# Three pairs of k-tiles for two in a kernel that takes seven block products for eight, with the weight sums written in place

## The chip, the cores and the metric

The kernel runs on one core of a Trainium2 chip. The metric is the device time of one execution in microseconds (us); it is the median of several runs.

## The reference

Four layers over 256 tokens of width 2048, in float32: an S5 layer with a gated unit, a dilated attention layer, each with a SwiGLU feed-forward network (FFN) behind it, and then two mixer layers (retention, differential attention, a linear recurrence). What this case is about is the gated unit and the two FFNs:

```python
D_MODEL = 2048
D_FF = -(-8 * D_MODEL // (3 * 256)) * 256          # 5632

def swiglu_ffn(h, w_gate_up, w_down):
    gate, up = jnp.split(h @ w_gate_up, 2, axis=-1)
    return (jax.nn.silu(gate) * up) @ w_down

# gated unit of the S5 layer
val, gate = jnp.split(g @ w_glu, 2, axis=-1)
return (val.astype(f32) * jax.nn.sigmoid(gate.astype(f32))).astype(u.dtype)
```

## The kernel before

All weights are float32 in HBM and are read once. For a matrix product each operand is split in two float32r parts, `hi` (a cast on ACT) and `lo` (the difference, on DVE), and a product is three matmuls of 128x128 by 128x512: hi by hi, hi by lo, lo by hi. The activations lie transposed in `act_hi` and `act_lo` as 16 k-tiles of 128 rows by 256 tokens; the tokens are two halves of 128. PSUM has four banks `psg` for these products and four banks `psm` for the rest.

`gemm` (L55) is the plain product of 512 columns. `Strassen.gemm_pair` (L136) takes 1024 columns as two halves of 512 (the gate and the up columns of one chunk, or two neighbouring column blocks of `w_down`). For four of the k-tiles, as two pairs, it uses the Winograd form of Strassen's scheme: the two token halves, the two k-tiles of a pair and the two column halves make a 2 by 2 block product, which takes seven block products (L180 to L187) for eight. Their left operands are blocks of the activations or the sums made by `forms` (L109), made once for each set of activations; the right operands are three blocks of the weights (b11, b21, b22) and four sums (t3 = b22 - b12, t1 = b12 - b11, t2 = b22 - t1, t4 = b21 - t2) made by `total` (L153, its instruction L155) into a pool tile `wt` with three buffers. `split` (L127) makes `whi` (L132) and `wlo` (L133) of each of the seven; `product` (L158) issues the matmuls (L166 to L168); `kept` copies four intermediate results out of PSUM. The raw weights of this part are one tile `wraw4` with one buffer, loaded by L148.

The other twelve k-tiles go the direct way, in six groups of two (L204 to L222): a group is loaded into a tile of the pool `wraw`, which has two buffers (WB), each of its k-tiles is split into one `whi` and one `wlo` tile (four buffers each), and 12 matmuls follow on each. In the last group the order is by token half, so the banks c21 and c22 are done first. Then four adds (L230) put the kept parts back, or, for the down product, the caller adds them to `x` one by one (L376).

Between the seven products and the direct groups `jobs` runs what is waiting in `k.jobs`. In `ffn` this is `turn`: the gated chunk `midt` is transposed into `mid` (L269 to L274), and for the first chunk of a block of four the sums `mf` for the down product are made.

The order of instructions on each engine isn't the order of the program: a planner, which runs when the program is built, starts an instruction when its operands and its buffers are there by its own clock, and earlier lines go first. Buffers of a pool tile with one name go round. At the chip each engine then runs its list in that order.

`ffn` (L323) has eleven chunks of 512 in blocks of four, four and three: a first chunk by `gemm`, ten gate/up pairs, and two down pairs for each block. `glu` has three pairs.

## Time and profile before

| | us |
|---|---|
| median of 3 runs | 3208.32 (3207.38 to 3209.45) |
| profiled execution | 3209.36 |
| its span | 3207.6 |
| PE busy | 3137.0 |
| DVE busy | 2277.0 |
| ACT busy | 1728.8 |

The mean granted clock of the TensorE is 0.996 of full speed. Lines with an L number are those of the kernel; numbers of buffers are left out of names, so `wraw` stands for the pool of the direct groups and for `wraw4` alike. A time that begins a row of a timeline is in us from the start of the span.

### The profile page before, as it was taken

Reading aid. Unit: us, or ns where it says so; the run is one execution under the profiler, and the core shown is the slowest. Engines: PE = TensorE matmul, PEld = TensorE weight load, DVE = VectorE, ACT = ScalarE, POOL = GpSimd, SP = SyncE. Lnnn points to the kernel's source line nnn. Section 1 sums busy time; section 2 is a strip of 40 time slices with the busy share of each in tenths; the row PEclk is TensorE's granted clock in tenths of the full one; section 3 lists DMA queues with packets and bytes.
Section 4 is the critical chain, followed back from the end, with each engine's and each line's share of the span. In section 5 each row is a group of like instructions: output and inputs, shape, how many; then the busy total and the mean of one; then the engine's idle time right before and its main releaser. Section 6 shows DMA issues by size and latency. Waiting matters only on the chain.

```text
span 3207.6 us, 43406 instructions
## 1 busy us (share of the span) xinstructions
PE 3137.0 (98%) x16872; PEld 2671.6 (83%) x16883; DVE 2277.0 (71%) x3421; ACT 1728.8 (54%) x2335; POOL 13.8 (0%) x23
## 2 busy tenths in 40 slices
PE   4999999999999999999999999999999999999998
PEld 4788888888888888888888888888889898899887
DVE  8967777777777665756768777777858566575564
ACT  6355655455555655545455555545556455564463
POOL 1000000000000000000000000000000000000000
PEclk9999999999999999999999999999999999999999
DMA  3265655665555555454565565566555557456554
GB/s 55 85 216 171 210 182 186 209 210 194 200 197 178 171 168 177 163 189 158 168 204 186 195 201 184 182 207 210 184 162 166 184 152 221 158 165 202 155 182 170
DMA packets 343215, 573.96 MB, mean 179 GB/s; under 512 B 55073, under 2 KB 106785, under 8 KB 342177
## 3 DMA queue, kind: packets, MB, share of 16 engines
q1 hardware_dynamic: 309344, 561.91, 53.5%
q10 hardware_dynamic: 33664, 9.28, 1.4%
q8 instruction: 132, 2.16, 0.3%
q14 instruction: 75, 0.61, 0.1%
HBM read 568.51 MB, written 2.62 MB: 178 GB/s over the span
## 4 chain that ended last, share of the span: by engine, by line
PE 91%; DVE 3%; ACT 3%; DMA 2%; issue 0%; SPq 0%; ACTq 0%; another core or an unknown queue 0%; DVEq 0%
PE psg L71 14%; PE psg L69 14%; PE psg L70 14%; PE psg L220 11%; PE psg L221 11%; PE psg L222 11%; PE psg L166 4%; PE psg L167 3%; PE psg L168 3%; PE psm L269 1%; PE psg L399 1%; DMA wraw<-in_w_in 1%; DVE S L399 1%; PE psm L1044 1%; DVE sc L399 1%; ACT VW L399 1%
## 5 line engine op out<-in xcount | busy, mean ns | idle before, releaser
L43 DVE TENSOR_TENSOR wlo<-wraw,whi 128x1024 fp32r<-128x1024 f32 (+1 forms) x560 | 628.1, 1131 | 467.9 <-ACT whi L42 466.6
L42 ACT CAST whi<-wraw 128x1024 fp32r<-128x1024 f32 (+1 forms) x560 | 540.8, 978 | 640.1 <-PE psg L71 377.1
L133 DVE TENSOR_TENSOR wlo<-wraw,whi 128x1024 fp32r<-128x1024 f32 x509 | 608.4, 1222 | 279.5 <-ACT whi L132 277.1
L69 PE MATMUL psg<-whi,act_hi 128*128 128x512 f32 (+1 forms) x2144 | 802.8, 374 | 0.9 <-DVE act_lo L399 0.7
L71 PE MATMUL psg<-whi,act_lo 128*128 128x512 f32 (+1 forms) x2144 | 796.4, 372 | 4.1 <-DVE act_lo L279 4.1
L70 PE MATMUL psg<-wlo,act_hi 128*128 128x512 f32 (+1 forms) x2144 | 796.2, 371 | 0.8 <-DVE wlo L43 0.8
L132 ACT CAST whi<-wraw 128x1024 fp32r<-128x1024 f32 x509 | 522.8, 1055 | 488.7 <-DMA wraw<-in_w_gate_up 168.5
L220 PE MATMUL psg<-whi,act_hi 128*128 128x512 f32 x1616 | 630.8, 390 | 0.8 <-ACT whi L132 0.8
L221 PE MATMUL psg<-wlo,act_hi 128*128 128x512 f32 x1616 | 628.9, 389 | 0.8 <-DVE wlo L133 0.8
L222 PE MATMUL psg<-whi,act_lo 128*128 128x512 f32 x1616 | 628.8, 389 | 0.0
L71 PEld LDWEIGHTS psg<-whi,act_lo 128*128 128x128 f32 x2144 | 403.2, 188 | 59.9 <-DVE act_lo L279 5.0
L69 PEld LDWEIGHTS psg<-whi,act_hi 128*128 128x128 f32 x2144 | 403.6, 188 | 55.6 <-issue 1.3
L70 PEld LDWEIGHTS psg<-wlo,act_hi 128*128 128x128 f32 x2144 | 403.7, 188 | 53.7 <-DVE wlo L43 1.5
L220 PEld LDWEIGHTS psg<-whi,act_hi 128*128 128x128 f32 x1616 | 303.4, 188 | 63.6 <-ACT whi L132 1.2
L221 PEld LDWEIGHTS psg<-wlo,act_hi 128*128 128x128 f32 x1616 | 303.4, 188 | 63.4 <-DVE wlo L133 1.1
L222 PEld LDWEIGHTS psg<-whi,act_lo 128*128 128x128 f32 x1616 | 303.3, 188 | 63.1
L132 ACT CAST whi<-wt 128x1024 fp32r<-128x1024 f32 x140 | 147.7, 1055 | 119.7 <-PE psg L222 101.7
L133 DVE TENSOR_TENSOR wlo<-wt,whi 128x1024 fp32r<-128x1024 f32 x140 | 170.8, 1220 | 50.4 <-ACT whi L132 50.3
L155 DVE TENSOR_TENSOR wt<-wraw 128x1024 f32<-128x1024 f32 x70 | 84.3, 1220 | 8.4 <-DMA wraw<-in_w_down 6.7
L155 DVE TENSOR_TENSOR wt<-wraw,wt 128x1024 f32<-128x1024 f32 x70 | 85.5, 1221 | 1.1
L168 PE MATMUL psg<-whi,act_lo 128*128 128x512 f32 x210 | 82.0, 390 | 0.0
L167 PE MATMUL psg<-wlo,act_hi 128*128 128x512 f32 x210 | 81.9, 390 | 0.0
(359 smaller groups left out, 2931.6 us busy)
## 6 DMA issues: line engine op xcount, KB each, us to landing
wraw<-in_w_gate_up SPq DMA_DIRECT2D x320, 512.0 KB, 4.7
wraw<-in_w_down SPq DMA_DIRECT2D x176, 512.0 KB, 5.1
wraw<-in_w_in SPq DMA_DIRECT2D x96, 768.0 KB, 4.7
wraw<-in_w_q SPq DMA_DIRECT2D x48, 1024.0 KB, 5.1
wraw<-in_w_kv SPq DMA_DIRECT2D x32, 1024.0 KB, 5.5
wraw<-in_w_in SPq DMA_DIRECT2D x32, 1024.0 KB, 5.0
wraw<-in_w_out SPq DMA_DIRECT2D x32, 1024.0 KB, 5.1
wraw<-in_w_glu SPq DMA_DIRECT2D x48, 512.0 KB, 4.7
```

What stands on the lines that cost most here:

```text
L42: k.act_at = nc.scalar.copy(hi[:, :n, :cw], raw[:, a:a + n, :cw]).ins
L43: k.dve_at = nc.vector.tensor_tensor(lo[:, :n, :cw], raw[:, a:a + n, :cw], hi[:, :n, :cw].bitcast(F32), ALU.subtract).ins
L69: nc.tensor.matmul(o, a, wh, start=n == 0, stop=False)
L70: nc.tensor.matmul(o, a, wl, start=False, stop=False)
L71: k.mm = nc.tensor.matmul(o, b, wh, start=False, stop=n == total - 1).ins
L132: k.act_at = nc.scalar.copy(hi, src).ins
L133: k.dve_at = nc.vector.tensor_tensor(lo, src, hi.bitcast(F32), ALU.subtract).ins
L167: nc.tensor.matmul(o, a, wl[:, q], start=False, stop=False, skip_group_check=True)
L168: k.mm = nc.tensor.matmul(o, b, wh[:, q], start=False, stop=q == 1, skip_group_check=True).ins
L220: nc.tensor.matmul(o, a, wh[:, n], start=False, stop=False, skip_group_check=True)
L221: nc.tensor.matmul(o, a, wl[:, n], start=False, stop=False, skip_group_check=True)
L222: k.mm = nc.tensor.matmul(o, b, wh[:, n], start=False, stop=g == last and j == 1, skip_group_check=True).ins
```

## The change

The seven products take three pairs of k-tiles in all pairs but the down pairs of layer 1, which keep two; five direct groups remain for six. A block of weights is now two pieces, of two pairs and of one (`sizes`), each with its own raw tile, its own sums and its own `whi` and `wlo` tile, of which the second uses half. t1 is written over b11, t3 over b12, t4 over t2; t2 has a tile of its own for each piece. The product with b21 stands ahead of that with t4. The sums of the activations are made by `fill` in pieces too, and the room for that is no longer two `wt` buffers but one buffer of `wraw`; the piece of two pairs is filled after the first chunk of a block, that of one pair after the second. `midt` has one buffer for two, and so has `sil` in layer 1.

```diff
@@ -103,32 +103,36 @@
     def __init__(self, k, pool):
         self.k, self.pool = k, pool
 
-    def block(self):
-        return self.pool.tile([128, 2, 512], F32, name="wt", bufs=3)
-
-    def forms(self, xT, kt0, name):
+    def new_forms(self, kt0, name, sizes=(2, 1)):
+        return (kt0, sizes, *(self.pool.tile([128, 4, sum(sizes), 128], F32R, name=f"{name}_{n}") for n in ("hi", "lo")))
+
+    def fill(self, forms, xT, groups=None):
 
         k, nc = self.k, self.k.nc
-        xh, xl = (x[:, kt0:kt0 + 4, :] for x in xT)
-        hi, lo = (self.pool.tile([128, 4, 2, 128], F32R, name=f"{name}_{n}") for n in ("hi", "lo"))
-        x = self.block().rearrange("p q (i t) -> p (q i) t", i=2)
-        nc.vector.tensor_tensor(x, xh.bitcast(F32), xl.bitcast(F32), ALU.add)
-        x = x.rearrange("p (q i) t -> p q i t", i=2)
-        a11, a12, a21, a22 = (x[:, :, i, t * 128:(t + 1) * 128] for t in range(2) for i in range(2))
-        sm = self.block().rearrange("p a (b t) -> p (a b) t", t=128).rearrange("p (f q) t -> p f q t", q=2)
-        nc.vector.tensor_tensor(sm[:, 0], a21, a22, ALU.add)
-        nc.vector.tensor_tensor(sm[:, 2], a11, a21, ALU.subtract)
-        nc.vector.tensor_tensor(sm[:, 1], sm[:, 0], a11, ALU.subtract)
-        nc.vector.tensor_tensor(sm[:, 3], a12, sm[:, 1], ALU.subtract)
-        nc.scalar.copy(hi, sm)
-        nc.vector.tensor_tensor(lo, sm, hi.bitcast(F32), ALU.subtract)
-        return kt0, hi, lo
+        kt0, sizes, hi, lo = forms
+        for g in range(len(sizes)) if groups is None else groups:
+            m, q0 = sizes[g], sum(sizes[:g])
+            room = k.wraw.tile([128, 4, 512], F32, name="wraw")
+            xh, xl = (x[:, kt0 + 2 * q0:kt0 + 2 * (q0 + m), :] for x in xT)
+            h, l = (f[:, :, q0:q0 + m, :] for f in (hi, lo))
+            x = room[:, 0:m].rearrange("p q (i t) -> p (q i) t", i=2)
+            nc.vector.tensor_tensor(x, xh.bitcast(F32), xl.bitcast(F32), ALU.add)
+            x = x.rearrange("p (q i) t -> p q i t", i=2)
+            a11, a12, a21, a22 = (x[:, :, i, t * 128:(t + 1) * 128] for t in range(2) for i in range(2))
+            sm = room[:, 2:2 + m].rearrange("p a (b t) -> p (a b) t", t=128).rearrange("p (f q) t -> p f q t", q=m)
+            nc.vector.tensor_tensor(sm[:, 0], a21, a22, ALU.add)
+            nc.vector.tensor_tensor(sm[:, 2], a11, a21, ALU.subtract)
+            nc.vector.tensor_tensor(sm[:, 1], sm[:, 0], a11, ALU.subtract)
+            nc.vector.tensor_tensor(sm[:, 3], a12, sm[:, 1], ALU.subtract)
+            nc.scalar.copy(h, sm)
+            nc.vector.tensor_tensor(l, sm, h.bitcast(F32), ALU.subtract)
 
     def split(self, src):
 
         k, nc = self.k, self.k.nc
-        hi = k.whi.tile([128, 2, 512], F32R, name="whi")
-        lo = k.wlo.tile([128, 2, 512], F32R, name="wlo")
+        m = src.shape[1]
+        hi = k.whi.tile([128, 2, 512], F32R, name="whi")[:, :m, :]
+        lo = k.wlo.tile([128, 2, 512], F32R, name="wlo")[:, :m, :]
         k.act_at = nc.scalar.copy(hi, src).ins
         k.dve_at = nc.vector.tensor_tensor(lo, src, hi.bitcast(F32), ALU.subtract).ins
         return hi, lo
@@ -139,33 +143,42 @@
 
 
         k, nc = self.k, self.k.nc
-        kt0, sh, sl = forms
+        kt0, sizes, sh, sl = forms
+        pairs = sum(sizes)
         xh, xl = xT
-        raw = self.pool.tile([128, 2, 2, 2, 512], F32, name="wraw4")
-        for n, c0 in enumerate(cols):
-            for q in range(2):
-                r0 = row0 + (kt0 + 2 * q) * 128
-                nc.sync.dma_start(raw[:, q, :, n, :], W[r0:r0 + 256, c0:c0 + 512].rearrange("(i p) c -> p i c", p=128))
-        b11, b12, b21, b22 = (raw[:, :, i, n, :] for i in range(2) for n in range(2))
+        raws = []
+        for g, m in enumerate(sizes):
+            raws.append(self.pool.tile([128, m, 2, 2, 512], F32, name=f"sraw{g}"))
+            for n, c0 in enumerate(cols):
+                for q in range(m):
+                    r0 = row0 + (kt0 + 2 * (sum(sizes[:g]) + q)) * 128
+                    nc.sync.dma_start(
+                        raws[g][:, q, :, n, :], W[r0:r0 + 256, c0:c0 + 512].rearrange("(i p) c -> p i c", p=128)
+                    )
+        b11, b12, b21, b22 = ([r[:, :, i, n, :] for r in raws] for i in range(2) for n in range(2))
         c22, c21, c11, c12 = (k.psg.tile([128, 512], F32, name="psg") for _ in range(4))
         blocks = {"A11": (0, 0), "A12": (1, 0), "A22": (1, 1)}
 
-        def total(a, b):
-            t = self.block()
-            nc.vector.tensor_tensor(t, a, b, ALU.subtract)
-            return t
+        def less(outs, a, b):
+            for g in range(len(sizes)):
+                nc.vector.tensor_tensor(outs[g], a[g], b[g], ALU.subtract)
+            return outs
 
         def product(o, form, w, start):
-            wh, wl = self.split(w)
-            for q in range(2):
-                if form in blocks:
-                    i, t = blocks[form]
-                    a, b = (x[:, kt0 + 2 * q + i, t * 128:(t + 1) * 128] for x in xT)
-                else:
-                    a, b = (x[:, int(form[1]) - 1, q, :] for x in (sh, sl))
-                nc.tensor.matmul(o, a, wh[:, q], start=start and q == 0, stop=False, skip_group_check=True)
-                nc.tensor.matmul(o, a, wl[:, q], start=False, stop=False, skip_group_check=True)
-                k.mm = nc.tensor.matmul(o, b, wh[:, q], start=False, stop=q == 1, skip_group_check=True).ins
+            q0 = 0
+            for m, src in zip(sizes, w):
+                wh, wl = self.split(src)
+                for q in range(m):
+                    if form in blocks:
+                        i, t = blocks[form]
+                        a, b = (x[:, kt0 + 2 * (q0 + q) + i, t * 128:(t + 1) * 128] for x in xT)
+                    else:
+                        a, b = (x[:, int(form[1]) - 1, q0 + q, :] for x in (sh, sl))
+                    end = q0 + q == pairs - 1
+                    nc.tensor.matmul(o, a, wh[:, q], start=start and q0 + q == 0, stop=False, skip_group_check=True)
+                    nc.tensor.matmul(o, a, wl[:, q], start=False, stop=False, skip_group_check=True)
+                    k.mm = nc.tensor.matmul(o, b, wh[:, q], start=False, stop=end, skip_group_check=True).ins
+                q0 += m
 
         def kept(o, name):
             e = self.pool.tile([128, 512], F32, name=name)
@@ -174,19 +187,21 @@
 
         product(c22, "A11", b11, True)
         p1 = kept(c22, "st_p1")
-        product(c21, "S3", total(b22, b12), True)
+        t1 = less(b11, b12, b11)
+        t3 = less(b12, b22, b12)
+        t2 = less([self.pool.tile([128, m, 512], F32, name=f"wt{g}") for g, m in enumerate(sizes)], b22, t1)
+        product(c21, "S3", t3, True)
         p7 = kept(c21, "st_p7")
-        t1 = total(b12, b11)
-        t2 = total(b22, t1)
         product(c22, "S2", t2, False)
         u2 = kept(c22, "st_u2")
-        product(c21, "A22", total(b21, t2), False)
+        t4 = less(t2, b21, t2)
         product(c11, "A12", b21, True)
+        product(c21, "A22", t4, False)
         product(c22, "S1", t1, False)
         u4 = kept(c22, "st_u4")
         product(c12, "S4", b22, True)
 
-        direct = [kt for kt in kts if not kt0 <= kt < kt0 + 4]
+        direct = [kt for kt in kts if not kt0 <= kt < kt0 + 2 * pairs]
         calls = 1 + len(direct) // 4
         called = 0
 
@@ -322,7 +337,7 @@
 @with_exitstack
 def ffn(ctx, k, layer):
     nc, I = k.nc, k.I
-    work = ctx.enter_context(k.tc.tile_pool(name="ffnw", bufs=2))
+    work = ctx.enter_context(k.tc.tile_pool(name="ffnw", bufs=1))
     st = Strassen(k, ctx.enter_context(k.tc.tile_pool(name="strassen", bufs=1)))
     dff = I["w_down"].shape[1]
     gain = load_gain(k, I["ffn_norm"][layer])
@@ -330,15 +345,16 @@
     rstd = x_stats(k)
     wgu, wd = I["w_gate_up"][layer], I["w_down"][layer]
     nch = dff // 512
-    mforms = []
+    forms = st.new_forms(KT - 6, "xf")
     for s0 in range(0, nch, 4):
         n = min(4, nch - s0)
         mid = act_pair(k, 0)
+        mforms = st.new_forms(0, "mf", (2, 1)[:2 - layer])
         for c in range(s0, s0 + n):
             m = work.tile([128, 2, 512], F32, name="midt")
 
             def silu(t, g):
-                sil = work.tile([128, 512], F32, name="sil")
+                sil = work.tile([128, 512], F32, name="sil", bufs=2 - layer)
                 nc.scalar.activation(sil, g, AF.Silu, scale=rstd[:, t:t + 1])
                 return sil
 
@@ -348,7 +364,7 @@
             if c == 0:
                 pg = gemm(k, xT, kgroups(), wgu, 0, 512)
                 sils = [silu(t, pg[t]) for t in range(2)]
-                forms = st.forms(xT, 12, "xf")
+                st.fill(forms, xT)
                 pu = gemm(k, xT, kgroups(), wgu, dff, 512)
                 for t in range(2):
                     gated(t, pu[t], sils[t])
@@ -357,17 +373,17 @@
                 for t in (1, 0):
                     gated(t, ps[t][1], silu(t, ps[t][0]))
 
-            def turn(m=m, c=c, s0=s0):
+            def turn(m=m, c=c):
                 split_transposed(
                     k, lambda t, i: m[:, t, i * 128:(i + 1) * 128], mid, [4 * (c - s0) + i for i in range(4)]
                 )
-                if c == s0:
-                    mforms.append(st.forms(mid, 0, "mf"))
+                if c - s0 < len(mforms[1]):
+                    st.fill(mforms, mid, (c - s0,))
 
             meanwhile(k, turn)
         for nn in range(0, 4, 2):
             pd, rest = st.gemm_pair(
-                mid, mforms[-1], range(4 * n), wd, s0 * 512, (nn * 512, nn * 512 + 512), apart=True
+                mid, mforms, range(4 * n), wd, s0 * 512, (nn * 512, nn * 512 + 512), apart=True
             )
             for of in (rest, pd):
                 for t in (1, 0):
@@ -933,7 +949,8 @@
         load_x(k)
     k.lo_at = k.sp_at = None
     sig = [sigmoid(t, pg[t]) for t in range(2)]
-    forms = st.forms(gT, 12, "xf")
+    forms = st.new_forms(KT - 6, "xf")
+    st.fill(forms, gT)
     pv = gemm(k, gT, groups, w, 0, 512)
     for t in range(2):
         gated(0, t, pv[t], sig[t])
```

## Rows read from the trace of the kernel before

**Rows 1.** The page: chain of work that ended last, by engine.

```profile
PE 91%; DVE 3%; ACT 3%; DMA 2%; issue 0%; SPq 0%; ACTq 0%; another core or an unknown queue 0%; DVEq 0%
```

**Rows 2.** The chain in order of time: start us, us, what.

```profile
476.10 0.87 PE psm L269 x8
519.22 0.87 PE psm L269 x8
```

**Rows 3.** Timeline of PE in a direct stretch: start us, us, what.

```profile
477.05 0.40 PE L221 MATMUL psg<-wlo,act_hi 128*128 128x512 f32 x1
...
502.90 0.39 PE L221 MATMUL psg<-wlo,act_hi 128*128 128x512 f32 x1
```

**Rows 4.** Busy time by stretch: from:to, us, PE, PEld, DVE, ACT, POOL, clock, DMA.

```profile
509.47:519.05 9.58, 9.58 (x43) 7.84 (x42) 9.58 (x11) 9.01 (x12) 0.00 (x0) 1.00 0.09 24
519.05:552.58 33.53, 33.53 (x153) 27.91 (x152) 24.63 (x26) 13.65 (x15) 0.00 (x0) 1.00 0.74 244
```

**Rows 5.** Timeline of DVE to the next seven products; in brackets idle before, and releaser.

```profile
489.19 1.23 DVE L155 TENSOR_TENSOR wt<-wraw 128x1024 f32<-128x1024 f32 x1 [0.45 <-DMA wraw<-in_w_down]
490.33 1.22 DVE L133 TENSOR_TENSOR wlo<-wraw,whi 128x1024 fp32r<-128x1024 f32 x1
491.47 1.22 DVE L155 TENSOR_TENSOR wt<-wraw 128x1024 f32<-128x1024 f32 x1
492.72 1.23 DVE L155 TENSOR_TENSOR wt<-wraw,wt 128x1024 f32<-128x1024 f32 x1
...
502.59 1.23 DVE L133 TENSOR_TENSOR wlo<-wraw,whi 128x1024 fp32r<-128x1024 f32 x1 [1.49 <-ACT whi L132]
...
507.65 1.21 DVE L155 TENSOR_TENSOR wt<-wraw,wt 128x1024 f32<-128x1024 f32 x1
508.79 0.74 DVE L346 SCALAR_TENSOR_TENSOR midt<-psg,rstd,sil 128x512 f32<-128x512 f32 x1
509.45 0.69 DVE L230 TENSOR_TENSOR psg<-psg,st_p 128x512 f32<-128x512 f32 x1
510.05 0.69 DVE L230 TENSOR_TENSOR psg<-psg,st_u 128x512 f32<-128x512 f32 x1
510.64 1.21 DVE L133 TENSOR_TENSOR wlo<-wt,whi 128x1024 fp32r<-128x1024 f32 x1
```

**Rows 6.** Groups by line over the whole span: count, then busy us, mean ns, idle before.

```profile
L155 DVE TENSOR_TENSOR wt<-wraw,wt 128x1024 f32<-128x1024 f32 x70 | 85.5, 1221 | 1.1
L155 DVE TENSOR_TENSOR wt<-wraw 128x1024 f32<-128x1024 f32 x70 | 84.3, 1220 | 8.4 <-DMA wraw<-in_w_down 6.7 <-DMA wraw<-in_w_gate_up 1.6
```

**Rows 7.** Timeline of ACT in the same direct stretch.

```profile
483.84 2.00 ACT L132 CAST whi<-wraw 128x1024 fp32r<-128x1024 f32 x2 [5.63 <-DMA wraw<-in_w_gate_up]
...
492.58 2.00 ACT L132 CAST whi<-wraw 128x1024 fp32r<-128x1024 f32 x2 [3.62 <-DMA wraw<-in_w_gate_up]
...
501.51 1.05 ACT L132 CAST whi<-wraw 128x1024 fp32r<-128x1024 f32 x1 [1.67 <-PE psg L222]
```

**Rows 8.** Timeline of DVE behind a pair whose job makes the sums `mf`.

```profile
393.68 1.23 DVE L115 TENSOR_TENSOR wt<-act_hi,act_lo 128x1024 f32<-128x1024 f32 x1
...
399.95 1.22 DVE L124 TENSOR_TENSOR mf_lo<-wt,mf_hi 128x1024 fp32r<-128x1024 f32 x1
```

**Rows 9.** Timeline of SP's queue; then GB/s in 40 slices of 466 to 510.

```profile
473.97 0.88 SPq L148 DMA_DIRECT2D wraw<-in_w_down  x2
476.24 4.28 SPq L208 DMA_DIRECT2D wraw<-in_w_gate_up  x4
...
496.25 5.76 SPq L208 DMA_DIRECT2D wraw<-in_w_down  x4
...
GB/s 0 0 0 0 0 0 0 0 171 236 387 341 339 385 404 380 356 372 331 101 97 326 408 147 123 363 397 71 65 330 344 214 19 227 330 246 155 0 0 0
```

**Rows 10.** Timeline of PE behind a hole, and the clock (as rows 4) after it.

```profile
2780.49 2.82 PE L269 MATMUL psm<-ident,x 128*128 128x128 f32 x12 [3.94 <-DVE x L1546]
...
2781.00:2786.00 5.00, 5.00 (x22) 4.91 (x21) 4.80 (x11) 4.52 (x15) 0.00 (x0) 0.50 0.58 157
```

## The prediction

> **What bounds the kernel now.** I began with the page: PE is busy for 3137 of 3207.6 us, and the chain that ended last is PE for 91% of the span [rows 1]. The chain in order of time then gives the rhythm: the eight transposes that close each seven-product part stand 43.11 us apart, again and again [rows 2]. A timeline of PE shows why: between 477.05 and 502.90 there are 114 steps from one 128x512 matmul to the next, so 25.85 / 114 = 0.2267 us each, with no hole [rows 3]. One gate/up pair has 42 matmuls in seven products and 144 direct ones; 186 x 0.2267 + 0.87 of transposes = 43.0 us. So in the pairs PE is the bound, and a matmul saved is 0.2267 us saved, if its operands are on time.
>
> Whether they are is read from the other engines around the start of a seven-product part (509.47). In the part itself, to 519.05, DVE is busy throughout (9.58 of 9.58 us), while in the direct stretch it is busy 24.63 of 33.53 [rows 4]. So DVE just keeps up in the seven products: its difference for t2 starts at 510.64, lasts 1.21, and PE wants it at about 512.4. It keeps up because three of the four weight sums (the L155 instructions at 489.19, 491.47 and 492.72) run 17 to 20 us before the part begins, in DVE's slack; only t4 (507.65) runs late [rows 5].
>
> **What is saved.** The two groups of L155 count 70 + 70 instructions, four to a pair, so 35 pairs: 3 in the gated unit, 16 in each FFN [rows 6]. Six of them (the down pairs of layer 1, where `mf` keeps two k-pairs) keep their size. In 29 pairs a third k-pair takes seven products for eight: one product of three matmuls less, 87 in all, 87 x 0.2267 = 19.7 us. (The Trainium skill, "TensorE: Matmul & The Clock Gate", section "Wait - 56ns, not 53.3ns?", gives N / 2.4 GHz + 2.5 ns, which is 215.7 ns at N = 512; the trace has 226.7 ns at a granted clock of 1.0, and the measurement decides. By the page the gain would be 18.8 us.)
>
> **What is added on DVE, and where it falls.** A 1024-column difference or sum starts 1.14 us after the one before it when nothing is waited for, a 512-column one 0.60 (adds at 509.45, 510.05, 510.64), the gated product 0.66 [rows 5]. Every sum and split of a product is now a 1024 and a 512 instruction: 1.74 us for 1.14. ACT's casts and copies have the smaller sum and are left out.
>
> The order matters more than the amount. t1 is now written over b11, so it must follow both the cast and the difference of b11; t3 is written over b12, which t1 reads; t2 reads t1. All three, which ran 17 us ahead, now stand behind b11's split. That split can't move ahead: `whi` has four buffers, handed out in program order. The trace shows it: the direct stretch ends at 509.47 and each of its twelve tiles is 12 matmuls, 2.72 us, so the fifth tile gave its buffer back at 509.47 - 7 x 2.72 = 490.4; b11's weights had landed by 489.19 (the sum t3, read from the same loads, ran then), yet ACT stood until 492.58 for the next direct tile; b11's cast came last, at 501.51, released by PE, its difference at 502.59 [rows 5, 7]. In the new order b11's first half takes the buffer of the fourth tile before it likewise, so it starts 6.9 us before the seven products, as now.
>
> From there, DVE has to do, before the first 1024 columns of b22 are ready: six splits and two thirds of the seventh, 7 x 1.74 - 0.60 = 11.6; four sums, 7.0; the epilogue of the pair before, four adds and two gated products, 2.4 + 1.3 = 3.7 (its inputs come only at the end of the direct stretch, so it can't move out). Sum 22.3, so at best done at 22.3 - 6.9 = 15.4 us. PE, unhindered, begins the seventh product after six of nine matmuls, at 54 x 0.2267 = 12.24, and wants the difference one matmul later, at 12.47. **DVE is 2.9 us late even without a hole.** A list by hand, with sums ahead of splits as the planner placed them before, has holes: the next pair's first product waits 0.5 us for the gated product to free its PSUM bank, t3's difference comes 2.3 us late behind t1, t3, t2 and the epilogue, b21's 1.2 late behind t4: 4.0 us. I take 4.0, bounds 2.9 and 5.0 (one further hole like the 1.49 us that DVE stands idle ahead of 502.59 [rows 5], less what it overlaps).
>
> By what comes before the pair: after a gate/up or gated-unit pair, 19 pairs (2 + 10 + 7), 76 us (55 to 95). After a down pair the epilogue at that place is four adds to `x`, put at the same 0.60, and no gated products, 1.3 less: 7 pairs at 2.7, 19 us (11 to 28). After a plain gemm, two gated products: 3 pairs at 1.6, 5 us (1.5 to 9). The six down pairs of layer 1 get the new order without the saving: 7 x 1.14 + 4.6 + 3.7 - 6.9 = 9.4 against 8.4 wanted, so three at 2.0 and three at 0.5, 7.5 us (3 to 12). Sum 107 us (70 to 144).
>
> (The Trainium skill, "VectorE: DVE Perf Modes", section "The DRAIN you can't avoid", has the next instruction wait until the pipe is empty; then each would cost its full 1.22 or 0.69 us and the list would be about 2 us longer per pair. The starts in the trace stand 1.14 and 0.60 apart, so I don't follow it.)
>
> **The scratch room in `wraw`.** `fill` takes a whole buffer of `wraw`, which has two. In `turn` it stands, in program order, between the seven products and the direct groups, so group g0 can get its buffer only after the room, whose first write needs the transposed activations. In the old form the same work runs from 393.68 (L115) to 399.95 + 1.22 (L124), 7.5 us with splits between [rows 8]. Now g0's and g1's loads, today issued 13 and 8 us before the seven products begin (496.25 and, within that entry, up to 502.0 [rows 9]), fall behind it. g0's load is queued on SP behind loads of the next pair's raw blocks, which wait for b22's split, 2.3 us before the seven products end. With four of those ahead (2 MB) and its own 1 MB (3.1 million bytes in all) at about 370 GB/s (331 to 408 in the busy slices [rows 9]) that is 8.5 us of transfer, and some 1.6 us lie between the issue at 473.97 and the first busy slice, so it lands 2.3 us before plus 10.1, 7.8 us after the end of the seven products; the cast takes 1.05, so PE starts 8.1 us late and then waits about 1 us more for the difference: 9.0. If g0 slips in early instead, g1 still waits for the room: its chain, counted from the transposes (0.87, then cast and difference to 2.3, then L115 to L124 at their row lengths, 5.2), ends at 7.5, a load lands about 5 later, and PE wants it at 6.3: still 5.5 to 8. With all six raw loads ahead: 12. Today's nearest row: the g2 load of 476.24 with two raw loads ahead is first cast at 483.84, 7.6 us later [rows 7, 9]. There are nine such places (two in each of three blocks in layer 0, one in each of layer 1): 9 x 9.0 = 81 us (50 to 108). The three fills beside plain gemms find PE 10.9 us (four tiles) behind the splits: nothing, and a few us if that cover is short.
>
> After 3.94 us without a matmul the granted clock was 0.50 from 2781 to 2786 [rows 10]: the lower of the two levels. Holes of 8 us should bring that back each time: half of some 4 us of matmuls, 2 us, nine times 18 us (0 to 31).
>
> The other edits: one `midt` and one `sil` buffer fewer hold nothing up, since each is read before the next is written at these distances; with one `sil` in layer 1 the first chunk's second activation waits for a gated product, 0.7 us, once.
>
> **Sum.** The profiled execution took 3209.4 us (span 3207.6), 0.03% over the median of the runs. 3209.4 - 19.7 + 107 + 81 + 18 = 3395.7; say **3395 us**. Its own bounds: 3209.4 - 19.7 + 70 + 50 + 0 = 3310 and 3209.4 - 19.7 + 144 + 108 + 31 = 3473.
>
> **Rivals.** (1) The room costs nothing: the planner grants `wraw`, which DMAs fill, to whichever is ready first, while `whi` stays in order. g0 and g1 are then loaded ahead as now, and the sum is 3209.4 - 19.7 + 107 = 3297 (3260 to 3334). For it: nothing in this trace shows an order on `wraw`. Against it: `whi` shows one [rows 7]. 18%. (2) The sums cost little and the room all: b11's halves, with smaller casts, get in ahead of the last direct tiles, and t1 to t3 use DVE's slack: 3209.4 - 19.7 + 81 + 18 = 3289. 6%. (3) **Faster:** buffers of every name go to whichever is ready, so both costs vanish and PE stays the bound: 3209.4 - 19.7 = 3190. It decides at b11's cast: at 498 or earlier (2.9 us or more ahead of today's 501.5) the sums are hidden. For it: DVE has 8.9 us of slack in a direct stretch [rows 4], and the weights are there at 489 [rows 5]. Against it: ACT stood idle from 489 to 492.58 with b11's weights and a buffer there [rows 7]. 11%, of which 2% with a remainder that brings it within 0.2% of the time before. (4) Worse than 3470, if all six raw loads stand ahead of g0 and the low clock lasts: 2%. The forecast has 63%.
>
> That the change doesn't do what it says can be seen only in the six down pairs that keep two k-pairs; they are counted so.
>
> The range leaves out (3), (4) and the ends of the others: 3260 to 3470. Within 0.2% (6.4 us) is about what a measurement can't tell from no change. Faster 9%, same 2%, slower 89%.
>
> **What the profile after would show.** Saving: 183 matmuls per gate/up pair at 0.2267. Sums: holes in PE inside the seven products, released by DVE's differences, about 4 us per pair; DVE dense from b11's difference to b22's; pairs with no fill 46.3 us apart for 43.1. Room: holes of 8 to 9 us before the direct groups in exactly nine pairs, released by a DMA of w_gate_up, g0's load issued after the next pair's raw loads; pairs 55 us apart; granted clock 0.5 behind them. Wrong if the pairs stand 42.4 us apart: then rival 3. If only the nine are missing, rival 1.

## The result and the profile after

| | us | against the kernel before (95% interval) |
|---|---|---|
| before, median of 4 runs | 3207.85 (3206.01 to 3209.45) | 1 |
| after, median of 4 runs | 3440.78 (3439.43 to 3445.34) | 1.0729 (1.0710 to 1.0747) |
| after, profiled execution and its span | 3440.37, 3438.6 | |

The change makes the kernel 7.3% slower; 3395 was forecast, with 3260 to 3470 as the range. The mean granted clock fell from 0.996 to 0.973. The page of after, instructions busy and the chain by engine (for [rows 1]):

```profile
PE 3210.1 (93%) x16796; PEld 2685.4 (78%) x16796; DVE 2415.7 (70%) x3718; ACT 1792.6 (52%) x2486; POOL 13.6 (0%) x23
...
PE 68%; DVE 14%; DMA 7%; ACT 5%; issue 4%; SPq 1%; ACTq 0%; POOL 0%; DVEq 0%; POOLq 0%
```

There are 16796 weight loads, one to a matmul, for 16883 before: the 87 that were to be saved. And yet PE's share of the chain went from 91% to 68%. What PE waits for, over the whole span (line waited at and releaser: us in total, times, longest):

```profile
PE psg L235 <- ACT whi L136: 77.6, 9, 9.6
PE psg L178 <- ACT whi L136: 49.5, 53, 2.5
...
PE psg L179 <- DVE wlo L137: 16.2, 17, 2.9
```

The first row is the room: nine waits ahead of the first direct matmul (L235). The other two lie in the seven products. Stage by stage (from:to, us, busy of PE, PEld, DVE, ACT, POOL, then clock, DMA share, GB/s; for [rows 4]): a seven-product part, the hole and the direct part of a pair with `fill`, and the next seven products.

```profile
454.21:473.54 19.33, 16.82 (x64) 12.78 (x63) 16.41 (x20) 11.29 (x16) 0.00 (x0) 0.91 0.06 13
473.54:483.05 9.51, 1.05 (x9) 0.79 (x7) 3.58 (x9) 2.79 (x5) 0.00 (x0) 0.71 1.04 391
483.05:512.82 29.77, 29.73 (x120) 23.96 (x121) 18.81 (x19) 12.52 (x13) 0.00 (x0) 0.92 0.65 221
512.82:532.17 19.35, 16.84 (x64) 12.76 (x63) 17.67 (x22) 13.26 (x19) 0.00 (x0) 0.91 0.06 13
```

63 matmuls at 0.2267 are 14.28 us; the part takes 19.35. DVE ahead of it and in it (for [rows 5]):

```profile
505.94 1.22 DVE L137 TENSOR_TENSOR wlo<-sraw,whi 128x1024 fp32r<-128x1024 f32 x1 [1.49 <-ACT whi L136]
507.20 1.22 DVE L164 TENSOR_TENSOR sraw<-sraw 128x1024 f32<-128x1024 f32 x1
...
508.94 1.22 DVE L164 TENSOR_TENSOR sraw<-sraw 128x1024 f32<-128x1024 f32 x1
...
515.00 1.81 DVE L164 TENSOR_TENSOR wt<-sraw 128x1024 f32<-128x1024 f32 x2
516.73 1.82 DVE L137 TENSOR_TENSOR wlo<-sraw,whi 128x1024 fp32r<-128x1024 f32 x2
518.47 1.82 DVE L137 TENSOR_TENSOR wlo<-wt,whi 128x1024 fp32r<-128x1024 f32 x2
```

The sums, which stood 17 to 20 us ahead, come behind b11's difference (505.94): t1, t3, and t2 only at 515.00, when PE is already at t3's product; t3's difference follows at 516.73. ACT's cast of t2 waits for that late sum. ACT, then PE there:

```profile
516.30 1.57 ACT L136 CAST whi<-wt 128x1024 fp32r<-128x1024 f32 x2 [0.61 <-DVE wt L164]
```

```profile
514.86 0.40 PE L178 MATMUL psg<-whi,xf_hi 128*128 128x512 f32 x1
517.40 0.51 PE L178 MATMUL psg<-whi,xf_hi 128*128 128x512 f32 x1 [2.14 <-ACT whi L136]
...
518.59 0.63 PE L178 MATMUL psg<-whi,xf_hi 128*128 128x512 f32 x1
519.02 0.63 PE L179 MATMUL psg<-wlo,xf_hi 128*128 128x512 f32 x1
...
521.58 0.56 PE L180 MATMUL psg<-whi,xf_lo 128*128 128x512 f32 x1
```

A hole of 2.3 us (2.54 from start to start, less 0.2267). What ended it is the cast of t2, whose first matmul PE's list has at 517.40, ahead of the rest of t3's; the first difference of t3 was there only at 517.95. Behind it, from 518.59 to 521.58, matmuls start 0.43 apart for 0.2267: the lower clock level (the granted clock of 518.59 to 521.98 is 0.51). The room, first SP's queue, then ACT (for [rows 7, 9]) and PE:

```profile
471.26 1.91 SPq L155 DMA_DIRECT2D sraw<-in_w_gate_up  x4
473.29 6.74 SPq L223 DMA_DIRECT2D wraw<-in_w_gate_up  x4
```

```profile
481.96 1.99 ACT L136 CAST whi<-wraw 128x1024 fp32r<-128x1024 f32 x2 [3.56 <-DMA wraw<-in_w_gate_up]
```

```profile
473.55 1.04 PE L284 MATMUL psm<-ident,midt 128*128 128x128 f32 x8
483.05 1.22 PE L235 MATMUL psg<-whi,act_hi 128*128 128x512 f32 x2 [8.47 <-ACT whi L136]
```

g0's load stands behind four raw loads here, as forecast, and PE stands 8.47 us.

The whole difference of the spans, 231.0 us, from the starts of PE's matmuls in all 35 pairs of both kernels:

| | us | forecast |
|---|---|---|
| 87 matmuls saved | -19.7 | -19.7 |
| seven products, above their matmuls: waits | 108 | 107 |
| seven products, half clock (133 matmuls at 0.42 to 0.48 apart) | 27 | 0 |
| nine holes ahead of the direct groups | 80 | 81 |
| direct groups longer behind them | 19 | 18 |
| between the pairs, 12 of it around the plain gemm of each layer's first chunk | 14 | 0 to a few |
| before the first and behind the last pair | 3 | 0 |

### The profile page after: what moved, and what is told of

Read it like the earlier page. It is cut to its first block, busy times and chain, and to the rows that moved or that the text cites. A ratio compares the mean times of both kernels' runs of the same rounds, so it can differ in the third digit from the quotient of the medians.

```text
span 3438.6 us, 43829 instructions
## 1 busy us (share of the span) xinstructions
PE 3210.1 (93%) x16796; PEld 2685.4 (78%) x16796; DVE 2415.7 (70%) x3718; ACT 1792.6 (52%) x2486; POOL 13.6 (0%) x23
## 4 chain that ended last, share of the span: by engine, by line
PE 68%; DVE 14%; DMA 7%; ACT 5%; issue 4%; SPq 1%; ACTq 0%; POOL 0%; DVEq 0%; POOLq 0%
PE psg L71 12%; PE psg L70 12%; PE psg L69 12%; DVE wlo L137 6%; PE psg L235 5%; PE psg L236 5%; PE psg L237 5%; DMA wraw<-in_w_gate_up 4%; ACT whi L136 3%; PE psg L179 3%; PE psg L180 3%; PE psg L178 3%; DMA wraw<-in_w_down 2%; DVE sraw L164 2%; PE psm L415 1%
## 5 line engine op out<-in xcount | busy, mean ns | idle before, releaser
L137 DVE TENSOR_TENSOR wlo<-wraw,whi 128x1024 fp32r<-128x1024 f32 x346 | 411.1, 1222 | 322.1 <-ACT whi L136 321.6
L235 PE MATMUL psg<-whi,act_hi 128*128 128x512 f32 x1384 | 546.3, 396 | 77.6 <-ACT whi L136 77.6
L136 ACT CAST whi<-wraw 128x1024 fp32r<-128x1024 f32 x346 | 350.9, 1050 | 394.0 <-DMA wraw<-in_w_gate_up 202.2
L236 PE MATMUL psg<-wlo,act_hi 128*128 128x512 f32 x1384 | 546.4, 395 | 0.4
L237 PE MATMUL psg<-whi,act_lo 128*128 128x512 f32 x1384 | 544.5, 393 | 0.0
L69 PEld LDWEIGHTS psg<-whi,act_hi 128*128 128x128 f32 x2144 | 404.7, 189 | 65.7 <-ACT whi L42 8.9
L136 ACT CAST whi<-sraw 128x1024 fp32r<-128x1024 f32 x320 | 267.4, 855 | 241.4 <-PE psg L237 86.2
L235 PEld LDWEIGHTS psg<-whi,act_hi 128*128 128x128 f32 x1384 | 263.2, 191 | 133.8 <-ACT whi L136 79.7
L137 DVE TENSOR_TENSOR wlo<-sraw,whi 128x1024 fp32r<-128x1024 f32 x320 | 302.7, 978 | 48.3 <-ACT whi L136 48.1
L178 PE MATMUL psg<-whi,xf_hi 128*128 128x512 f32 x276 | 117.6, 426 | 32.8 <-ACT whi L136 32.7
L179 PE MATMUL psg<-wlo,xf_hi 128*128 128x512 f32 x276 | 121.7, 441 | 9.7 <-DVE wlo L137 9.0
L178 PE MATMUL psg<-whi,act_hi 128*128 128x512 f32 x297 | 119.8, 403 | 10.2 <-ACT whi L136 8.9
L164 DVE TENSOR_TENSOR sraw<-sraw 128x1024 f32<-128x1024 f32 (+1 forms) x128 | 124.9, 978 | 1.4
```

The source lines that it names most:

```text
L69: nc.tensor.matmul(o, a, wh, start=n == 0, stop=False)
L136: k.act_at = nc.scalar.copy(hi, src).ins
L137: k.dve_at = nc.vector.tensor_tensor(lo, src, hi.bitcast(F32), ALU.subtract).ins
L178: nc.tensor.matmul(o, a, wh[:, q], start=start and q0 + q == 0, stop=False, skip_group_check=True)
L179: nc.tensor.matmul(o, a, wl[:, q], start=False, stop=False, skip_group_check=True)
L235: nc.tensor.matmul(o, a, wh[:, n], start=False, stop=False, skip_group_check=True)
```

## The experiments

Theory: two costs that add, sums behind b11's split and the room that stands ahead of g0. Rivals: the amount of DVE's work in three pairs, not its order; `fill`'s own chain; the larger raw loads.

**The room apart.** `fill` works in the tile `wt{g}`, in place:

```diff
-            room = k.wraw.tile([128, 4, 512], F32, name="wraw")
+            x = self.pool.tile([128, m, 512], F32, name=f"wt{g}").rearrange("p q (i t) -> p (q i) t", i=2)
...
-            nc.vector.tensor_tensor(sm[:, 0], a21, a22, ALU.add)
+            nc.vector.tensor_tensor(a22, a21, a22, ALU.add)
```

> One part undone: `fill` no longer takes a buffer of `wraw`; it works in place in the tiles `wt0` and `wt1` (same six DVE and ACT instructions per piece, same place in the program). The weight sums stay as in the kernel after (3440.8 us). Theory (the room shares a two-buffer pool with g0 and g1 and stands before them): all that belongs to the room goes, 79.7 us of holes before the direct groups, 20.8 us of low clock behind them, 11 to 12 us beside the plain gemms: 3440.8 - 112 = 3329 us (3315 to 3345), the hole at the nine places below 1 us, the seven-product parts unchanged at 19.3 us. Rival (the holes come from the chain of `fill` itself, whose DVE and ACT work stands ahead of g0's splits wherever its room is): holes of about 5 us stay, 3440.8 - 9 x 4 = 3405 us. Rival (the three raw pairs, 3 MB for 2 MB, crowd the DMA queue and g0 comes late for that): no gain, 3430 to 3441.

Measured 3332.5 us (1.0389, 1.0373 to 1.0404): 108 less than after. PE goes from the transposes to the direct groups without a hole, and these run at full clock:

```profile
453.89 1.04 PE L282 MATMUL psm<-ident,midt 128*128 128x128 f32 x8
454.68 0.47 PE L233 MATMUL psg<-whi,act_hi 128*128 128x512 f32 x1
```

```profile
454.68:481.99 27.31, 27.31 (x123) 22.62 (x122) 19.78 (x25) 11.91 (x15) 0.00 (x0) 1.00 0.83 289
```

The 14 us between the pairs fell to 2. So this share is the shared pool, not `fill`'s instructions (which are all still there) and not the larger loads.

**Sums ahead.**

```diff
-        t1 = less(b11, b12, b11)
+        t1 = less([self.pool.tile([128, m, 512], F32, name=f"wt{g}") for g, m in enumerate(sizes)], b12, b11)
         t3 = less(b12, b22, b12)
-        t2 = less([self.pool.tile([128, m, 512], F32, name=f"wt{g}") for g, m in enumerate(sizes)], b22, t1)
+        t2 = less(b11, t3, b11, ALU.add)
```

> The other part undone, as far as it costs no memory: t1 goes to the tile `wt`, so t1 and t3 (over b12) need nothing but the loads and can run ahead; t2 = t3 + b11 is written over b11 behind its split, t4 over t2. Same number of DVE instructions. The room stays in `wraw`. Theory (t1, t3 and t2 behind b11's split make DVE late): DVE has 22.3 - 3.5 = 18.8 us of work from b11's difference to b22's, less the 6.9 of lead = 11.9, and PE wants it at 12.47, so the stalls go but for up to 1 us a pair, and with them their low clock: the seven-product part falls from 19.35 to 14.3 to 15.5 us, total 3440.8 - 135 = 3306 us (to 3336 with 1 us a pair left). The nine holes before the direct groups stay at 9 us. Rival (it is the amount, 1.74 us for 1.14 in each of eleven steps, not the order): 3420 to 3441, seven-product part above 18.5 us.

Measured 3369.4 us (1.0503, 1.0488 to 1.0519): 71 less, where 105 to 135 were expected. A part of such a pair, and DVE in it:

```profile
513.43:529.44 16.01, 15.35 (x64) 11.64 (x63) 15.22 (x19) 13.28 (x20) 0.00 (x0) 1.00 0.07 17
```

```profile
518.44 1.82 DVE L164 TENSOR_TENSOR sraw<-sraw 128x1024 f32<-128x1024 f32 x2
520.18 3.56 DVE L137 TENSOR_TENSOR wlo<-sraw,whi 128x1024 fp32r<-128x1024 f32 x4
```

The part falls from 19.35 to 16.01 and the clock in it is back at 1.00. Of the 135 us in the seven products 82 go, 53 stay (1.5 a pair). The span fell by 67 only, since 15 us came back elsewhere, 6.5 of them ahead of the first pair. So neither "order alone" nor "amount alone" fits: t4 (518.44) still has to follow t2's split, and DVE is dense.

**Both.** The two edits together.

> Both parts undone together: room in `wt`, t1 in `wt` and ahead, t3 over b12, t2 over b11. Theory (two separate costs which add, and the saving of 87 matmuls stands behind them): 3440.8 - 112 - 135 = 3194 us, to 3224 if 1 us a pair stays in the seven products; against the kernel before (3207.9) a ratio of 0.9957 (to 1.005). Gate/up pairs 42.4 us apart (to 43.4), granted clock 0.995. Rival (the two overlap: a PE that is late in the seven products hides part of the room, or the other way round): 3230 to 3270.

Measured 3251.6 us (1.0142, 1.0125 to 1.0159): 189 less than after, and 108 + 71 = 179 by the two alone. So the two measured savings add, to within 10 us; 3252 lies in the rival's range only because the sums ahead gave 71 us for 135. What is left over 3194 is the 55 us above the matmuls in the seven products.

**The room's place in the order.** `turn` was cut in two, with `fill` one step of the queue later.

```diff
-                    st.fill(mforms, mid, (c - s0,))
+                    return lambda: st.fill(mforms, mid, (c - s0,))
```

> The kernel after with one thing moved: in `turn` the transposes stay where they are, and `fill` is handed out one step later, behind g1 in the program; its room is still a buffer of `wraw`. Sums as in the kernel after. Theory (buffers of a pool are given in the order of the program, so only the room's place ahead of g0 makes the hole): the nine holes go with their low clock, the fills beside the plain gemms stay: 3440.8 - 79.7 - 20.8 = 3340 us (3332 to 3360, the upper end if g3, which now waits for the room, comes up to 2 us late). Rival (two buffers are one too few for three users, wherever the third stands: the hole moves behind g1): 3380 to 3441, with holes of 4 us or more in the direct groups of the nine pairs.

Measured 3443.5 us (1.0738, 1.0716 to 1.0760). The edit moved nothing: the first call of `jobs` takes 8 x 1 // 3 = 2 steps, so both stayed ahead of g0. With one empty step between (the expectation says two; the edit puts in one, which is enough, since the first call takes two steps):

> What the edit before it was meant to do: there `jobs` takes two steps of the queue in its first call (8 x 1 // 3), so the sums were still handed out ahead of g0 and the run was a repeat of the kernel after (3443.5). Now two empty steps stand between, so that `fill` comes with the second call, behind g0 and g1 in the program; its room is still a buffer of `wraw`, the weight sums are as in the kernel after. Theory (buffers are given in the order of the program, so the room's place ahead of g0 makes the hole): the nine holes go with the low clock behind them, the fills beside the plain gemms stay: 3440.8 - 79.7 - 20.8 = 3340 us (3332 to 3360, the upper end if g2 or g3, which now follow the room, come up to 2 us late). Rival (two buffers are one too few for three users wherever the third stands): the hole moves behind g1, holes of 4 us or more in the direct groups of the nine pairs, 3380 to 3441.

Measured 3361.8 us (1.0476, 1.0461 to 1.0492): 79 less, just above the theory's 3332 to 3360. One of the nine places:

```profile
463.85 1.04 PE L289 MATMUL psm<-ident,midt 128*128 128x128 f32 x8
464.64 0.48 PE L235 MATMUL psg<-whi,act_hi 128*128 128x512 f32 x1
```

The nine holes are gone (0.80 us of transposes between the parts), with the room still in `wraw`; so it was its place ahead of g0. The rest went elsewhere: one direct part has a hole of 2.1 us behind the room (another has one of 3.0, but e1 and e3, without a room in `wraw`, have 2.3 and 2.7 us in the same pair), and the seven products next behind a pair with `fill` are 1 to 2 us longer.

**Two pairs, sums in place.** The kernel before, with t1 over b11, t3 over b12, t4 over t2, b21's product ahead of t4's:

```diff
+        t1 = total(b12, b11, b11)
+        t3 = total(b22, b12, b12)
+        t2 = total(b22, t1, self.block())
-        product(c21, "S3", total(b22, b12), True)
+        product(c21, "S3", t3, True)
...
-        product(c21, "A22", total(b21, t2), False)
+        t4 = total(b21, t2, t2)
         product(c11, "A12", b21, True)
+        product(c21, "A22", t4, False)
```

> The kernel before, with two pairs, one piece and its old rooms for the sums of the activations; alone the order of the weight sums is the new one: t1 over b11, t3 over b12, t2 and t4 in one `wt`, the product with b21 ahead of that with t4. No instruction more. Theory (order): t1, t3 and t2 stand behind b11's split; the layer-1 down pairs of the kernel after, which are just this, were 1.6 to 2.2 us longer in their seven products, so 35 x 1.8 = 63, 3208 + 63 = 3271 us (3255 to 3290). Rival (it is the amount, the 1.74 us for 1.14 of the third pair, that makes DVE late): 3208 to 3220.

Measured 3283.8 us (1.0233, 1.0218 to 1.0249): 75 more than before, without one instruction more on DVE. A seven-product part (9.57 us in the kernel before), and DVE around it:

```profile
477.85:489.79 11.94, 10.68 (x42) 7.67 (x43) 10.77 (x12) 9.06 (x12) 0.00 (x0) 1.00 0.03 6
```

```profile
470.40 1.23 DVE L133 TENSOR_TENSOR wlo<-wraw,whi 128x1024 fp32r<-128x1024 f32 x1 [1.49 <-ACT whi L132]
471.66 2.48 DVE L154 TENSOR_TENSOR wraw<-wraw 128x1024 f32<-128x1024 f32 x2
...
481.18 1.22 DVE L133 TENSOR_TENSOR wlo<-wraw,whi 128x1024 fp32r<-128x1024 f32 x1
482.31 1.22 DVE L154 TENSOR_TENSOR wt<-wraw,wt 128x1024 f32<-128x1024 f32 x1
```

So order alone costs 2.4 us behind a gate/up pair and 1.6 behind a down pair. The sums stand behind b11's difference (470.40), and t4 (482.31) behind t2's, where the kernel before had it before the part began. This run doesn't part the two, nor the swap of b21's product with t4's.

**All three sums ahead where memory allows.**

```diff
+        t2 = less(fresh("wu"), b22, t1) if self.roomy else less(b11, t3, b11, ALU.add)
```

> As e3_both (3251.6 us), but in the gated unit and in layer 0, where 6 KB per partition are free, t2 has a tile of its own too (`wu`), so that t1, t3 and t2 can all run ahead, as in the kernel before; in layer 1 t2 is still written over b11. In e3_both the 19 pairs of the gated unit and layer 0 are together 39.8 us over the 14.28 us of 63 matmuls in their seven products. Theory (order): DVE then has 22.3 - 5.2 = 17.1 us from b11's difference to b22's, less 6.9 of lead = 10.2, against 12.47: the excess falls to 0.3 a pair or less, 3251.6 - 34 = 3218 us (3210 to 3224); layer 1 unchanged. Rival (amount): sums that run ahead push b11's split later or leave splits of direct tiles late, excess stays above 1 us a pair, 3235 to 3252.

Measured 3247.5 us (1.0118, 1.0101 to 1.0135): only 4 less than with t2 late. The theory missed; t2's place was not what was left. Parts of 15.8 us stay, with a hole at b21's product behind t4's sum.

**The clock.** The kernel after, with 36 idle matmuls in each hole:

```diff
                 if c - s0 < len(mforms[1]):
+                    o = k.psm.tile([128, 2, 256], F32, name="psm").rearrange("p a b -> p (a b)")
+                    for _ in range(36):
+                        nc.tensor.matmul(o, xT[0][:, 0, 0:128], xT[0][:, 0:2, :].rearrange("p a b -> p (a b)"), start=True, stop=True)
                     st.fill(mforms, mid, (c - s0,))
```

> The kernel after, with 36 matmuls of 128x512 more behind the transposes wherever sums of a new block are made (nine pairs), into a PSUM bank that nobody reads: 36 x 0.2267 = 8.2 us of work in holes of 8.6 to 9.9. Nothing else is moved. Theory (the clock falls because PE stands idle, and the direct groups behind pay for it): the direct parts of the nine pairs fall from 29.2 to 30.5 back to 27.3 us, 3440.8 - 20.8 = 3420 us (3415 to 3428). Rival (the slow start of the direct groups is late operands, not the clock): direct parts as they were, 3436 to 3446.

Measured 3426.8 us (1.0682, 1.0666 to 1.0698): 14 less, not 21. The same hole and direct part as in after:

```profile
469.54:480.18 10.64, 9.22 (x46) 7.45 (x44) 3.59 (x9) 2.79 (x5) 0.00 (x0) 1.00 1.05 389
480.18:507.87 27.69, 27.62 (x121) 22.56 (x122) 18.63 (x19) 12.38 (x13) 0.00 (x0) 1.00 0.66 224
```

Clock 1.00 for 0.92, and 27.69 us for 29.77: the direct groups are slow for the clock, as forecast. 16 us of the direct time came back in the nine pairs together. But four of the holes grew by 1.0 to 1.2 us, 4.6 in all; these rows don't show why.

**t4 last.** Order b11, t3, b21, t2, t1, b22, t4, with t4's sum behind t1's splits.

> As e7_three_ahead (3247.5 us), with the seven products in another order: b11, t3, b21, t2, t1, b22, t4, and t4's sum behind the splits of t1, so that it no longer stands in front of b21's differences (in e7 DVE made t4 at 476.10 to 477.9 and b21's differences only behind it, and PE had its 0.72 us hole there). Number of instructions as before. Theory (what is left of the stall is a matter of order: the last sum made inside the seven products goes ahead of a split that PE wants sooner): the seven products of three-pair pairs fall from 15.8 to 14.4 to 14.8 us, 29 pairs x 1.0 to 1.4, and the down pairs of layer 1 from 11.9 to 9.8: 3247.5 - 40 = 3207 us (3200 to 3220), about the kernel before. Rival (amount: eleven steps of 1.74 us on DVE in 14.3 us are too many in any order): 3238 to 3250, seven products at 15.5 or more.

Measured 3238.8 us (1.0091, 1.0076 to 1.0107): 9 less, in the rival's range. A part, and DVE, ACT and PE in it:

```profile
469.99:485.62 15.63, 15.19 (x64) 11.64 (x63) 15.07 (x19) 13.28 (x19) 0.00 (x0) 1.00 0.19 60
```

```profile
476.58 1.22 DVE L162 TENSOR_TENSOR wu<-sraw,wu 128x1024 f32<-128x1024 f32 x1
477.71 1.82 DVE L135 TENSOR_TENSOR wlo<-wt,whi 128x1024 fp32r<-128x1024 f32 x2
```

```profile
477.94 1.05 ACT L134 CAST whi<-sraw 128x1024 fp32r<-128x1024 f32 x1 [0.53 <-PE psg L178]
```

```profile
479.04 0.99 PE L176 MATMUL psg<-whi,xf_hi 128*128 128x512 f32 x2 [0.44 <-ACT whi L134]
```

DVE is busy 15.07 of 15.63 us, and 1.35 us a pair above the matmuls are twice what a pair saves (3 x 0.2267 = 0.68). That fits the rival, the amount, but doesn't show it. In DVE's list the first piece of t4's sum (476.58) still stands ahead of t1's differences (477.71), so the order was reached only in part. And PE's one wait in the part is for a cast, for which ACT had stood until PE was done with an earlier tile: the number of split buffers may have a share. The mixers' tables one pair later (`range(16)` for `range(8)`):

> As e9_t4_last, and the small tables of the mixers, which DVE makes beside the first gate/up pair of layer 1, one pair later (16 empty steps for 8), where no sums `mf` are made. In e7 that pair was 49.89 us long for 43.25 in the kernel before, with a hole of 2.4 us behind a late difference of a direct tile. Theory (DVE is full there: tables, sums and splits): that pair falls to about 44, and the next is up by 1 to 2: e9_t4_last less 4 us (2 to 6). Rival (the tables cost the same wherever they are): the same as e9_t4_last within 2 us.

Measured 3232.2 us (1.0077, 1.0064 to 1.0090): 6.7 less, a little more than the 2 to 6 expected; the first gate/up pair of layer 1 fell from 48.58 to 43.63 us, and the next from 45.33 to 43.75, where 1 to 2 more were expected.

**t4 on POOL.** `less(t2, b21, t2, on=nc.gpsimd)`.

> As e10_t4_tables (3232.2 us), with the sum t4 on POOL, which is idle in this stretch, instead of on DVE. In e9 and e10 DVE is busy without a pause from the first adds of the epilogue to the last difference, and the seven products last 15.65 us for 14.28 of matmuls. Theory (the amount on DVE is what is left): 1.74 us a pair come off it, the seven products fall by 0.6 to 1.2 us where t4 is on time: 3232 - 29 x 0.9 = 3206 us (3197 to 3215), a little under the kernel before. POOL takes 0.42 to 0.62 us for 128x128 in the trace of before, so by columns 3.4 to 5.0 for 1024 and 1.7 to 2.5 for 512; t4 starts at about 7.6 us of the part and its second piece is done at 12.7 to 15.1, wanted at 13.6. Rival (POOL is too slow, or slows DVE beside it): PE waits for t4 at the last product, 3235 to 3275 us, DVE's instructions beside it longer than 1.14 and 0.60 apart.

Measured 3309.9 us (1.0299, 1.0284 to 1.0314): 78 more, beyond the rival's range too. POOL's sum of two pieces, and DVE's differences beside it:

```profile
484.35 4.95 POOL L162 TENSOR_TENSOR wu<-sraw,wu 128x1024 f32<-128x1024 f32 x2 [40.06 <-DVE wlo L135]
```

```profile
485.07 4.78 DVE L135 TENSOR_TENSOR wlo<-wt,whi 128x1024 fp32r<-128x1024 f32 x2 [0.25 <-ACT whi L134]
489.77 1.81 DVE L135 TENSOR_TENSOR wlo<-sraw,whi 128x1024 fp32r<-128x1024 f32 x2
```

The two differences take 4.78 us beside POOL and 1.81 when it is done: DVE loses 3.0 us to be spared 1.74.

**Split buffers for the small pieces.** Three pairs in 13 pairs only; pieces of one k-pair split into two buffers of their own.

```diff
+        if m == 1:
+            hi, lo = (self.pool.tile([128, 1, 512], F32R, name=n, bufs=2) for n in ("whi1", "wlo1"))
```

> Three pairs only in the 13 pairs of the gated unit and of layer 0's gate/up; all down pairs and all of layer 1 take two, with the products in the order of the kernel before and t2 in a tile of its own (the idle `sraw1`). The memory that this frees goes to the split: the pieces of one k-pair get two `whi` and two `wlo` buffers of their own, so that they no longer take one of the four. In the 13 pairs the products stand as in e9 (t2 over b11, t4 last), the room of `fill` is in `wt`. Theory (what is left in e9, 1.35 us a pair, is the number of split buffers: with four, DVE can put only b11 ahead of the seven products and then has 14 us of work in 14.3): with six, t3's first pieces are split before the part begins and the excess falls to 0.4 or less; the 13 pairs gain 3 x 0.2267 - 0.4 = 0.3 to 0.7 each, the rest is as before: 3208.5 - 4 to 9 = 3200 to 3205 us, faster than both. Rival (amount: DVE has too much in any case): seven products at 15.4 to 15.7 as in e9, 13 x 0.65 = 8 us lost, 3212 to 3220. Rival (the two-pair parts now lose by t3 over b12): down pairs and layer 1 above 43.3 us, 3215 to 3240.

Measured 3243.1 us (1.0110, 1.0093 to 1.0127), where 3200 to 3205 was expected. The 13 pairs do what the theory says in part: seven products of 14.66 us (0.4 above the matmuls, 1.1 in e10) behind plain gemms and down pairs, but 15.4 behind gate/up pairs (with one direct matmul in it, so 0.9 above, 1.3 in e10); against the kernel before a pair, counted from its start to that of the next, changed by -0.7 to +0.2 us, -0.5 in all. The other 22, with as many instructions as before, lost 37 us in all between their first and last matmul, 1.5 to 1.9 each in most and 4.2 in one: the second rival. DVE in one of them:

```profile
2010.82 1.22 DVE L138 TENSOR_TENSOR wlo<-sraw,whi 128x1024 fp32r<-128x1024 f32 x1
...
2012.55 1.22 DVE L165 TENSOR_TENSOR sraw<-sraw,sraw 128x1024 f32<-128x1024 f32 x1
```

Here t1, t3 and t2 did run ahead, but t4 (2012.55) is written over t2 and comes behind t2's split (2010.82). In the kernel before t4, in a third `wt` buffer, starts 3 us ahead of that split [rows 5]. I read this as what the 22 pairs lost; a t4 in a place of its own, or over b12 once t3 is split, wasn't tried.

## Why the prediction was right

**Saving.** 87 matmuls fewer, as counted. It is real but small, 0.68 us a pair, and no version here kept it: the 13 pairs of e12 come out even, all others pay more.

**Sums behind b11's split.** The term was 107 us, the waits came to 108. That it fits to 1 us is luck: behind gate/up and unit pairs they were 69 for 76, behind down pairs 23 for 19, behind plain gemms 6 for 5, in the six two-pair parts 11 for 7.5. A pair without `fill` showed much of the list made by hand: t3's hole, put at 2.3 us behind t1, t3, t2 and the epilogue, was 2.3, and 0.4 more until t3's difference was there. The sign named for it, holes that DVE's differences end, held for 16.2 us only; 49.5 us ended with a cast by ACT, which in the pair shown had waited for DVE's late sum. Moving t1 and t3 ahead took 82 of the 135 us with their clock. The reason was only part of it, though. Two-pair parts lost 1.6 to 2.4 us by order alone (e6), and still 1.5 to 1.9 with t1, t3 and t2 ahead and b21's product behind t4's (e12): t4 over t2, behind t2's split, looks like a cost of its own, which the prediction had in DVE's sum but not as a change of place. The prediction also took 6.9 us of lead for DVE as work that it can use; e2 and e7 had bounds of 11.9 and 10.2 us against 12.47 by that and were still 1.5 us late a pair. The lead was not usable in full: in e9, ahead of the part that starts at 469.99, DVE waits 0.65 and 0.49 us for PE to be done with the banks that the epilogue adds to.

```profile
466.79 0.70 DVE L246 TENSOR_TENSOR psg<-psg,st_u 128x512 f32<-128x512 f32 x1 [0.65 <-PE psg L238]
...
469.51 0.70 DVE L246 TENSOR_TENSOR psg<-psg,st_p 128x512 f32<-128x512 f32 x1 [0.49 <-PE psg L238]
```

**The room.** 81 us forecast, 80 found, in the nine places named, with g0's load behind four raw loads in the place shown. e1 shows the sharing and e5 the place in the order as its condition. Rivals 1 and 3, buffers granted by readiness, are out, and so is rival 2, sums that cost little.

**The low clock is the term that was too small.** 18 us stood for nine holes of 8 us, and the direct groups behind them lost 19. The "some 4 us" of slow matmuls in that term stood in no row of before ([rows 10] have the lower clock for 5 us); in after the granted clock of 483.05 to 487.05 was 0.50, and each of the nine direct parts took 1.8 to 3.0 us longer. Left out were the holes of 2.3 us in the seven products: 133 matmuls at half speed there, 27 us, gone in e2, where the longest hole of most parts is about 0.7 us. [rows 10] showed only a hole of 3.94 us. With the 14 us between the pairs, most of it beside the plain gemms, where the cover of four tiles was taken for enough, and 3 at the ends, that is nearly all of the 45 us by which 3395.7 was below 3440.4.

**Distances.** Gate/up pairs without `fill` stood 47.45 us apart for 46.3, those with it mostly 58.1 to 58.6 for 55: that clock again, in the seven products and, with `fill`, in the direct groups.

What stays open: how much of the last 1.4 us a pair is t4's place, how much the amount of DVE's work, and how much the number of split buffers (with two more of them, in e12, it was 0.4 to 0.9). The best version, 3232 us, is 0.8% slower than the kernel before.

## What to carry to other kernels

A sum that is written over its operand can't run before the last reader of that operand; in a kernel whose next engine is full around one stage, that moves work from slack into the stage, and here 7 block products for 8 didn't pay for it. A scratch tile taken from a pool that also feeds loads is a place in that pool's order: put it behind the loads that must run ahead, or elsewhere. Price each hole in PE with the slow matmuls behind it.

## What the hardware showed

DVE is slower beside POOL (e11): while POOL makes sums of 1024 and 512 columns (3.1 and 2.2 us in the mean), DVE's 1024-column difference took 2.63 us in the mean for 1.22, its 512-column one 1.55 for 0.68.

```profile
L135 DVE TENSOR_TENSOR wlo<-wt,whi 128x1024 fp32r<-128x1024 f32 x35 | 92.1, 2633 | 5.7 <-ACT whi L134 5.4
...
L135 DVE TENSOR_TENSOR wlo<-wu,whi 128x1024 fp32r<-128x1024 f32 x38 | 46.3, 1218 | 1.5 <-ACT whi L134 1.4
...
L135 DVE TENSOR_TENSOR wlo<-wt,whi 128x512 fp32r<-128x512 f32 x29 | 44.8, 1546 | 0.0
```

The middle row, of differences of t2 or t4, is the same size with POOL idle. No run has these sums on POOL with DVE idle, so what they cost POOL isn't shown.

And the clock of TensorE fell behind holes as short as 2.3 us, with PE busy on both sides (granted clock 0.91 over the part), while parts with holes of 0.7 to 1.0 us stayed at 1.00 (e2, e6). The length of the hole alone doesn't decide it: in another part of after the clock stayed at 1.00 with a hole of 2.6 us (958 to 960.7).

```profile
955.79:973.81 18.02, 15.27 (x65) 11.67 (x64) 17.28 (x22) 12.47 (x18) 0.00 (x0) 1.00 0.06 14
```
